# Attention values as 32-bit products in column halves, the causal mask on VectorE, and a mixed warm-up

## The chip, the core and the metric

The kernel runs on one core of a Trainium2 chip. A core has a matrix engine (TensorE, PE in the profile, with its weight loads listed as PEld), a vector engine (VectorE, DVE), an engine for activation functions and copies (ScalarE, ACT), a general engine (GpSimd, POOL) and a sync engine (SyncE, SP), which here issues nearly all DMAs. The engines run side by side, each in the order of its own queue, and wait for one another by semaphores. TensorE writes its products to PSUM (eight banks of 512 32-bit columns on 128 partitions); the other data sit in SBUF on 128 partitions.

The metric is the device time of one execution in microseconds. Before the change it is 1384.53 us, the median of three executions that lie between 1384.16 and 1384.84.

## The reference

One layer of a hybrid encoder for 1024 prompt frames and 32 frames of running streams that have 512 cached frames. All data are float32. Cut to what matters here:

```python
q, k, v, logf, ga, u, gb, ma, mb = mixer_inputs(x, ...)    # RMS norm and one wide projection
c = cumsum(logf)                                           # forget gates, per head
for i in range(T // 128):                                  # blocks of 128 queries
    s = q[block i] @ k[:hi].T + c[block i] - c[:hi]        # 16 heads of 64
    s = where(qpos >= kpos, s, -max)                       # causal mask
    o[block i] = softmax(s) @ v[:hi]
conv = causal_dwconv(u)                                    # 31 taps per channel
ya = (o * silu(ga)) @ w_pa
yb = (silu(layernorm(conv)) * silu(gb)) @ w_pb
y  = x + (sigmoid(ma) * ya + sigmoid(mb) * yb) @ w_out
```

Keys, values, log gates and the end of the convolution input are outputs too.

## The kernel before, in words

**Number formats.** A float32 product costs TensorE several passes. Most products here therefore take numbers in a rounded 32-bit format (the type `F32R`), which goes in one pass, and get their accuracy back by splitting an operand into a rounded high part and a low part (the rest), both of that type. A full product of two split operands is three one-pass products: high by high, low by high, high by low (`mms`, line 108).

**Stages.** The stages are: a start in which the tokens are normed and turned (`x_split`), with products on a zero tile ahead of it (`warm`, line 359) that keep TensorE occupied until the first tokens are there; projections for the convolution input, the values (line 600), keys and queries; a gate projection; then the attention stage; then the three output projections. The convolution taps run on VectorE beside the projections.

**Values in the projection stage.** For each group of four heads and each tile of 128 keys, ScalarE copies the values out of PSUM twice: as float32 (`vf`, line 606), which is stored as an output, and rounded (`vb`, line 608). Three steps later VectorE puts the low part beside the high one (line 613), and both are stored to `s_v` in DRAM, so that a key has 128 numbers per head: 64 high, 64 low.

**The attention stage.** `seq` holds 16 heads of 8 blocks (`Block(head, i)`: 128 queries, of which block i looks at i + 1 tiles of 128 keys), and four `Sample` items for the running streams, placed after block 0 of heads 3, 7, 11 and 15. TensorE's order is exactly the order of the loop (`manual_schedule`); the other engines' order is chosen by a planner. Iteration n of the loop does:

- `start(seq[n + 3])`, the scores of the block three further on: two products per half of the keys (lines 947 and 948) into one of two score buffers `psS` of two banks each, and then the mask as a bfloat16 product of an identity with a matrix of 0 and -1e30 on the last 128 keys (line 950). VectorE takes the row maximum (952), ScalarE the exponential and its row sum (955), GpSimd multiplies by the reciprocal (958).
- `turn()` of block n: TensorE transposes the probabilities in tiles of 128 (line 975) into a PSUM bank of the pool `psT` (three banks). ScalarE copies them out rounded (`pth`, 979), VectorE forms the low part (`ptl`, 980). Two blocks share one pair of tiles of 256 queries.
- `fill(4)`: four steps of a gate projection, of three 352-column products each (line 108). Eight steps make one chunk, whose result stands in the single bank of the pool `pq`; ScalarE copies it out (line 779) before the next chunk's first product may write there. So a chunk ends in every second fill. In head 8 three fills are left out.
- `values()` of block n - 2, for odd blocks alone: for the 256 queries of blocks i - 1 and i and for each of their key tiles, one product of V with `pth` and one with `ptl` (lines 991 and 992), 256 columns each. V is the stationary operand, 128 wide (64 high, 64 low), so the upper and lower 64 partitions of the result hold the two parts, which ScalarE (996) and VectorE (997) add into `ot`. For odd heads VectorE multiplies by the gate (1002), loaded when the head's first pair of blocks is done, and after block 7 the result is stored.

A head has 2 + 4 + 6 + 8 = 20 key tiles in its four pairs, so 40 value products; 16 heads have 640. V of the next head is loaded (one buffer) after the values of block 7.

Of the kernel before, what the change touches and what calls it, by code (L numbers as in the profile page):

```python
# [10 lines left out]
BF16 = mybir.dt.bfloat16  # L11
# [4 lines left out]
D = 1024  # L16
T = 1024
# [18 lines left out]
NWARM = 46  # L36
# [15 lines left out]
def build(tc, xT, xt, wv, wf, ckT, cv, clT, stT, vec, cst, yT, kT, vO, lfO, cpT, csT):  # L52
# [10 lines left out]
    s_v = dram.tile([8, 128, H, 128], F32, name="s_v")  # L63
# [281 lines left out]
    with tc.high_priority(offset=9000):  # L345
        nc.scalar.dma_start(cst_t[:, :C_CM], cst[:, :C_CM])
        load_tok(0)
        load_tok(1)
        nc.sync.dma_start(raws[0], wf[WIDX["ub", 0]])
        nc.sync.dma_start(vec_t, vec)  # L350
        nc.sync.dma_start(raws[1], wf[WIDX["ua", 0]])
        for t in range(2, 9):
            load_tok(t)
        nc.sync.dma_start(cst_t[:, C_CM:], cst[:, C_CM:])
        idle = xip.tile([128, CH], F32R, name="idle")
        nc.vector.memset(f32(idle), 0.0)
        warm = tr.tile([128, 512], F32, name="warm", tag="tr")
        for i in range(NWARM):
            nc.tensor.matmul(warm[:, :256], idle[:, :128], idle[:, :256], start=(i == 0), stop=(i == NWARM - 1))

# [7 lines left out]
    identb = cp.tile([128, 128], BF16, name="identb")  # L368
    cmaskb = cp.tile([128, 128], BF16, name="cmaskb")
# [115 lines left out]
    def consts():  # L485
        nc.vector.tensor_copy(smask, cst_t[:, C_SM:C_SM + TS])
        nc.vector.tensor_copy(identb, cst_t[:, C_ID:C_ID + 128])
        nc.vector.tensor_copy(cmaskb, cst_t[:, C_CM:C_CM + 128])
        nc.vector.tensor_copy(bones, cst_t[:, C_BO:C_BO + 128])
        nc.vector.tensor_scalar(qg8, vec_t[:, V_QG:V_QG + 1], 0.125, None, op0=ALU.mult)  # L490
# [86 lines left out]
    for c in range(4):  # L577
# [15 lines left out]
        for t in range(8):  # L593
# [18 lines left out]
            def low(ps=ps, vb=vb, t=t, c=c):  # L612
                nc.vector.tensor_sub(vb[:, :, 64:128], ps[:, :256].rearrange("p (h d) -> p h d", h=4),
                                     f32(vb[:, :, 0:64]))
                nc.sync.dma_start(s_v[t, :, 4 * c:4 * c + 4, :], f32(vb))

            later(3, low)
# [166 lines left out]
    class Head:  # L784
        def __init__(self, h):
            self.h = h

# [141 lines left out]
    class Block:  # L929
# [5 lines left out]
        def scores(self):  # L935
# [8 lines left out]
            for b in range(nb):  # L944
                last = b == nb - 1
                ksl = slice(b * w, b * w + wm)
                nc.tensor.matmul(ps[:, b, :wm], QB[:, qsl], KB[:, ksl], start=True, stop=False)  # L947
                nc.tensor.matmul(ps[:, b, :wm], QA[:, qsl], KA[:, ksl], start=False, stop=not last)  # L948
                if last:
                    nc.tensor.matmul(ps[:, b, w - 128:w], identb, cmaskb, start=False, stop=True)  # L950
# [9 lines left out]
        def turn(self):  # L960
            i, P = self.i, self.P
            if i % 2 == 0:
                tg = f"{(i // 2) % 2}"
                pth, ptl = [ap.tile([128, i + 2, 256], F32R, name=a, tag=a + tg, bufs=1) for a in ("pth", "ptl")]
                nc.gpsimd.memset(f32(pth[:, i + 1, 0:128]), 0.0)
                nc.gpsimd.memset(f32(ptl[:, i + 1, 0:128]), 0.0)
                self.head.p = pth, ptl
            self.p = self.head.p
            pth, ptl = self.p
            qo = slice((i % 2) * 128, (i % 2) * 128 + 128)  # L970
            for u in range((i + 4) // 4):
# [6 lines left out]
                js = slice(4 * u, 4 * u + nj)  # L978
                nc.scalar.copy(pth[:, js, qo], p3)  # L979
                nc.vector.tensor_sub(ptl[:, js, qo], p3, f32(pth[:, js, qo]))  # L980

        def values(self):
            if self.i % 2 == 0:
                return
            c, e = self.i // 2, self.head.h % 2
            pth, ptl = self.p
            V, ot = self.head.V, self.head.ot
            njb = 2 * c + 2
            po = psT.tile([128, 512], F32, name="po", tag="T")
            for j in range(njb):  # L990
                nc.tensor.matmul(po[:, :256], V[:, j, :], pth[:, j, :], start=(j == 0), stop=False)  # L991
                nc.tensor.matmul(po[:, :256], V[:, j, :], ptl[:, j, :], start=False, stop=(j == njb - 1))  # L992
            osl = slice(c * 256, c * 256 + 256)
            own = slice(64 * e, 64 * e + 64)
            oth = slice(64 - 64 * e, 128 - 64 * e)
            nc.scalar.copy(ot[own, osl], po[oth, :256])  # L996
            nc.vector.tensor_add(ot[own, osl], ot[own, osl], po[own, :256])  # L997
            if e == 1:
                if c == 0:
                    self.head.g = ap.tile([128, T], F32, name="ga", tag="kc", bufs=1)  # L1000
                    nc.sync.dma_start(self.head.g, s_g["ga"][self.head.h // 2, :, :T])
                nc.vector.tensor_mul(ot[:, osl], ot[:, osl], self.head.g[:, osl])
            if e == 1 and c == 3:
# [478 lines left out]
```

## Time and profile before

| What | Value |
|---|---|
| median of three executions | 1384.53 us |
| the profiled execution | 1384.38 us |
| its span, from the first to the last instruction | 1382.3 us |
| TensorE products busy | 1372.3 us (99%), 9478 instructions |
| VectorE busy | 975.5 us (71%) |
| ScalarE busy | 659.0 us (48%) |
| GpSimd busy | 654.7 us (47%) |
| attention stage, first to last value product | about 598 to 1088 us of the span |

The profile is a hardware trace of one execution. A group line reads: source line, engine, operation, tiles (`out<-in`), shapes, count, then busy time in us and mean duration of one in ns, then the idle time of the engine ahead of it and who ended it. In a timeline a row reads: start, duration, engine, line, operation, tiles, shapes, count. Products overlap one another in TensorE's pipeline, so the duration of one is longer than the time it takes from the next: to price a product in a stream, take the distance from its start to the next start.

### The profile page before, as it was taken

The numbers are of one execution on the slowest core, as the hardware profiler recorded it, in microseconds if no ns is written. First come the engines' busy times: TensorE is split into PE (matmuls) and PEld (weight loads), VectorE is DVE, ScalarE is ACT, GpSimd is POOL, SyncE is SP. The second block draws the span as 40 slices with busy tenths as digits, with TensorE's granted clock in tenths as the row PEclk, the third lists the DMA queues.
The fourth block names the chain that finished last, engine by engine and source line by source line (L and its number), as shares of the span: only waits on it lengthen the run. The fifth ranks groups of instructions, "written<-read, shape, count | busy, mean of one in ns | idle before, by whom it ended". The sixth has DMA issues, their size and how long they took to land.

```text
span 1382.3 us, 25127 instructions
## 1 busy us (share of the span) xinstructions
PE 1372.3 (99%) x9478; PEld 1333.4 (96%) x9478; DVE 975.5 (71%) x1368; ACT 659.0 (48%) x1346; POOL 654.7 (47%) x685
## 2 busy tenths in 40 slices
PE   8999999999999999999999999999999999999999
PEld 7999999999999999999999999999998999999999
DVE  6687788878898899747766667665454579255664
ACT  6333444556464642245555556655555566233320
POOL 2324244656585875453434343433433348355553
PEclk9999999999999999999999999999999999999999
DMA  5243442425242375245545456544552587634462
GB/s 214 63 174 124 147 144 93 154 70 168 94 158 94 118 195 162 77 136 151 152 124 163 126 171 173 143 136 138 151 153 94 181 318 258 210 110 138 138 202 68
DMA packets 113496, 203.36 MB, mean 147 GB/s; under 512 B 17696, under 2 KB 75936, under 8 KB 113376
## 3 DMA queue, kind: packets, MB, share of 16 engines
q1 hardware_dynamic: 113232, 201.70, 46.7%
q8 instruction: 75, 1.23, 0.4%
q14 instruction: 45, 0.37, 0.1%
q10 hardware_dynamic: 144, 0.07, 0.0%
HBM read 131.87 MB, written 69.84 MB: 146 GB/s over the span
## 4 chain that ended last, share of the span: by engine, by line
PE 95%; DMA 1%; DVE 1%; ACT 1%; issue 1%; POOL 0%; SPq 0%; ACTq 0%; POOLq 0%; DVEq 0%
PE pj L108 65%; PE pjv L600 7%; PE pj L1315 5%; PE ptr L975 5%; PE po L991 3%; PE po L992 3%; PE psS L947 3%; PE psS L948 2%; DMA xtok<-xt 1%; PE psS L950 1%; PE pst L724 1%; PE pst L723 1%; DMA raw<-wf 0%; PE ptx L442 0%; DMA u<-stT 0%
## 5 line engine op out<-in xcount | busy, mean ns | idle before, releaser
L108 PE MATMUL pj<-xh,wh 128*128 128x352 f32 (+2 forms) x1536 | 509.1, 331 | 1.7 <-ACT t L779 1.4
L108 PE MATMUL pj<-xl,wh 128*128 128x352 f32 (+2 forms) x1536 | 494.8, 322 | 0.2 <-DVE xl L445 0.2
L108 PE MATMUL pj<-xh,wl 128*128 128x352 f32 (+2 forms) x1536 | 493.1, 321 | 0.0
L100 POOL TENSOR_TENSOR wl<-raw,wh 128x384 fp32r<-128x384 f32 (+1 forms) x237 | 311.0, 1340 | 184.6 <-ACT wh L97 165.0
L272 DVE SCALAR_TENSOR_TENSOR y<-u,vec_t,y 128x1086 f32<-128x1086 f32 x240 | 378.4, 1577 | 11.5 <-ACT y L269 8.3
L108 PEld LDWEIGHTS pj<-xh,wh 128*128 128x128 f32 x1536 | 288.8, 188 | 4.7 <-ACT t L779 2.0
L108 PEld LDWEIGHTS pj<-xl,wh 128*128 128x128 f32 x1536 | 288.6, 188 | 1.4 <-DVE xl L445 1.2
L108 PEld LDWEIGHTS pj<-xh,wl 128*128 128x128 f32 x1536 | 289.2, 188 | 0.2 <-DVE wl L464 0.2
L958 POOL TENSOR_SCALAR P<-P,nm 128x128 f32<-128x128 f32 (+7 forms) x128 | 98.9, 773 | 228.8 <-DVE nm L957 195.8
L952 DVE TENSOR_REDUCE nm<-psS 128x1 f32<-128x128 f32 (+7 forms) x128 | 96.5, 755 | 72.2 <-PE psS L950 53.3
L979 ACT CAST pth<-ptr 128x512 fp32r<-128x512 f32 (+1 forms) x192 | 89.0, 481 | 81.6 <-PE ptr L975 81.3
L980 DVE TENSOR_TENSOR ptl<-ptr,pth 128x512 fp32r<-128x512 f32 (+1 forms) x192 | 103.3, 550 | 23.4 <-ACT pth L979 21.8
L97 ACT CAST wh<-raw 128x1024 fp32r<-128x1024 f32 x79 | 82.7, 1047 | 61.7 <-PE pj L108 28.5
L955 ACT ACTIVATE P<-psS,nm 128x128 f32<-128x128 f32 (+7 forms) x128 | 95.2, 744 | 35.0 <-DVE nm L952 31.4
L741 POOL TENSOR_TENSOR ql<-qn,qh 128x352 fp32r<-128x352 f32 (+1 forms) x48 | 64.3, 1340 | 69.1 <-ACT qh L740 59.8
L975 PE MATMUL ptr<-ident,P 128*128 128x128 f32 x576 | 85.0, 274 | 0.0
L991 PE MATMUL po<-pth,V 128*128 128x256 f32 x320 | 79.0, 283 | 0.0
L992 PE MATMUL po<-ptl,V 128*128 128x256 f32 x320 | 78.5, 281 | 0.0
L600 PE MATMUL pjv<-vwh,xh 128*128 128x260 f32 x256 | 72.5, 283 | 0.0
L600 PE MATMUL pjv<-vwl,xh 128*128 128x260 f32 x256 | 72.5, 283 | 0.0
L600 PE MATMUL pjv<-vwh,xl 128*128 128x260 f32 x256 | 72.3, 282 | 0.0
L997 DVE TENSOR_TENSOR ot<-ot,po 64x256 f32<-64x256 f32 x64 | 26.7, 417 | 59.9 <-ACT ot L996 59.2
(253 smaller groups left out, 2635.3 us busy)
## 6 DMA issues: line engine op xcount, KB each, us to landing
raw<-wf SPq DMA_DIRECT2D x92, 512.0 KB
s_v<-vb SPq DMA_DIRECT2D x32, 256.0 KB
QB<-s_q SPq DMA_DIRECT2D x32, 256.0 KB
KB<-s_k SPq DMA_DIRECT2D x32, 256.0 KB
V<-s_v SPq DMA_DIRECT2D x16, 512.0 KB
kT<-qn SPq DMA_DIRECT2D x8, 528.0 KB
s_ga<-t SPq DMA_DIRECT2D x24, 176.0 KB
s_gb<-t SPq DMA_DIRECT2D x24, 176.0 KB
```

The source lines that it names most:

```text
L100: nc.gpsimd.tensor_sub(wl[:, k0:k1, :], raw[:, k0:k1, :], f32(wh[:, k0:k1, :]))
L108: nc.tensor.matmul(ps, a[:, kt, :], b(kt, sl), start=(first and n == 0), stop=(last and n == N - 1))
L272: t = nc.vector.scalar_tensor_tensor(y, u[:, i:i + CW], w, y, op0=ALU.mult, op1=ALU.add)
L600: nc.tensor.matmul(ps[:, :VC], a, b, start=(n == 0), stop=(n == 23))
L952: nc.vector.tensor_reduce(nm[:, 0:1], ps[:, :nb, :w], axis=AX.XY, op=ALU.max, negate=True)
L955: nc.scalar.activation(P[:, :nk].rearrange("p (b w) -> p b w", b=nb), ps[:, :nb, :w], AF.Exp, bias=nm[:, 0:1], accum_out=nm[:, 1:2])
L958: nc.gpsimd.tensor_scalar(P[:, :nk], P[:, :nk], nm[:, 2:3], 1.0, op0=ALU.mult, op1=ALU.mult)
L975: nc.tensor.transpose(pt[:, 128 * j:128 * j + 128], P[:, 128 * (4 * u + j):128 * (4 * u + j) + 128], ident)
L979: nc.scalar.copy(pth[:, js, qo], p3)
L980: nc.vector.tensor_sub(ptl[:, js, qo], p3, f32(pth[:, js, qo]))
L991: nc.tensor.matmul(po[:, :256], V[:, j, :], pth[:, j, :], start=(j == 0), stop=False)
L992: nc.tensor.matmul(po[:, :256], V[:, j, :], ptl[:, j, :], start=False, stop=(j == njb - 1))
```

## The change

Four edits.

1. Values stay float32. The rounded copy `vb` and its low part are gone; `s_v` holds 64 numbers per key and head and is stored from `vf` at once. V is a float32 tile of 8 x 64.
2. The transposed probabilities stay float32, with one tile per pair of blocks (tag `pt0` with two buffers, `pt1` to `pt3` with one) instead of `pth` and `ptl`. They are copied out once: by ScalarE for the first four key tiles of a block, by VectorE for the others. All four pairs' value products come together at block 7: for key tile j one float32 product of V (64 wide) with 256 queries, into the lower 64 partitions for even j and into the upper 64 for odd j. The two PSUM banks taken hold two pairs each. Then the two partition halves are added, 512 queries at a time. The gate tile of an odd head is loaded at block 5.
3. The mask product is gone; VectorE adds a float32 mask to the last 128 key columns of the scores in PSUM, ahead of the row maximum.
4. The 46 warm-up products of 256 columns become 35 of 352, 256 and 512 columns, of two operands: the rounded 32-bit zero tile and a float16 zero tile.

```diff
-        for i in range(NWARM):
-            nc.tensor.matmul(warm[:, :256], idle[:, :128], idle[:, :256], start=(i == 0), stop=(i == NWARM - 1))
+        cold = xip.tile([128, 512], F16, name="cold")
+        nc.vector.memset(cold, 0.0)
+        kinds = [(idle, CH)] * 8 + [(cold, CH)] * 8 + [(idle, CH), (cold, CH)] * 4 + [(cold, 256)] * 6 + [(cold, 512)] * 5
+        for d, n in kinds:
+            nc.tensor.matmul(warm[:, :n], d[:, :128], d[:, :n], start=True, stop=True)
...
-            vb = vp.tile([128, 4, 128], F32R, name="vb", tag="vb", bufs=5)
-            nc.scalar.copy(vb[:, :, 0:64], ps[:, :256].rearrange("p (h d) -> p h d", h=4))
...
-            later(3, low)
+            nc.sync.dma_start(s_v[t, :, 256 * c:256 * c + 256], vf)
...
-            self.V = hp.tile([128, 8, 128], F32R, name="V", tag="V", bufs=1)
-            nc.sync.dma_start(f32(self.V), s_v[:, :, h, :].rearrange("b t d -> t b d"))
+            self.V = hp.tile([128, 8, 64], F32, name="V", tag="V", bufs=1)
+            nc.sync.dma_start(self.V, s_v[:, :, 64 * h:64 * h + 64].rearrange("b t d -> t b d"))
...
-                nc.tensor.matmul(ps[:, b, :wm], QA[:, qsl], KA[:, ksl], start=False, stop=not last)
-                if last:
-                    nc.tensor.matmul(ps[:, b, w - 128:w], identb, cmaskb, start=False, stop=True)
+                nc.tensor.matmul(ps[:, b, :wm], QA[:, qsl], KA[:, ksl], start=False, stop=True)
+            diag = ps[:, nb - 1, w - 128:w]
+            nc.vector.tensor_add(diag, diag, cmask)
...
             if i % 2 == 0:
-                tg = f"{(i // 2) % 2}"
-                pth, ptl = [ap.tile([128, i + 2, 256], F32R, name=a, tag=a + tg, bufs=1) for a in ("pth", "ptl")]
-                nc.gpsimd.memset(f32(pth[:, i + 1, 0:128]), 0.0)
-                nc.gpsimd.memset(f32(ptl[:, i + 1, 0:128]), 0.0)
+                c = i // 2
+                self.head.p[c] = ap.tile([128, i + 2, 256], F32, name="pt", tag=f"pt{c}", bufs=2 if c == 0 else 1)
+                nc.gpsimd.memset(self.head.p[c][:, i + 1, 0:128], 0.0)
...
-                nc.scalar.copy(pth[:, js, qo], p3)
-                nc.vector.tensor_sub(ptl[:, js, qo], p3, f32(pth[:, js, qo]))
+                (nc.vector.tensor_copy if u else nc.scalar.copy)(p[:, 4 * u:4 * u + nj, qo], p3)
 
         def values(self):
-            if self.i % 2 == 0:
+            if self.i == 5 and self.head.h % 2:
+                self.head.g = ap.tile([128, T], F32, name="ga", tag="kc", bufs=1)
+                nc.sync.dma_start(self.head.g, s_g["ga"][self.head.h // 2, :, :T])
+            if self.i < 7:
                 return
...
-            for j in range(njb):
-                nc.tensor.matmul(po[:, :256], V[:, j, :], pth[:, j, :], start=(j == 0), stop=False)
-                nc.tensor.matmul(po[:, :256], V[:, j, :], ptl[:, j, :], start=False, stop=(j == njb - 1))
+            pos = [psT.tile([128, 512], F32, name="po", tag="T") for _ in range(2)]
+            for c in range(4):
+                po = pos[c // 2][:, 256 * (c % 2):256 * (c % 2) + 256]
+                for j in range(2 * c + 2):
+                    rows = slice(64 * (j % 2), 64 * (j % 2) + 64)
+                    nc.tensor.matmul(po[rows], V[:, j, :], parts[c][:, j, :], start=(c % 2 == 0 and j < 2),
+                                     stop=(c % 2 == 1 and j >= 2 * c))
+            for u in range(2):
+                sl = slice(512 * u, 512 * u + 512)
+                nc.scalar.copy(ot[own, sl], pos[u][oth])
+                nc.vector.tensor_add(ot[own, sl], ot[own, sl], pos[u][own])
+                if e == 1:
+                    nc.vector.tensor_mul(ot[:, sl], ot[:, sl], self.head.g[:, sl])
```

In the small constants a float32 mask copy (`cmask`) takes the place of a bfloat16 identity and mask.

More of the change, by code (lines that the diff above doesn't have):

```diff
@@ L62, in build @@
     s_k = dram.tile([2, D, T], F32, name="s_k")
-    s_v = dram.tile([8, 128, H, 128], F32, name="s_v")
+    s_v = dram.tile([8, 128, D], F32, name="s_v")
     s_vs = dram.tile([TS, D], F32, name="s_vs")
@@ L367, in build @@
     smask = cp.tile([128, TS], F32, name="smask")
-    identb = cp.tile([128, 128], BF16, name="identb")
-    cmaskb = cp.tile([128, 128], BF16, name="cmaskb")
+    cmask = cp.tile([128, 128], F32, name="cmask")
     bones = cp.tile([128, 128], F32R, name="bones", tag="ob")
@@ L486, in consts @@
         nc.vector.tensor_copy(smask, cst_t[:, C_SM:C_SM + TS])
-        nc.vector.tensor_copy(identb, cst_t[:, C_ID:C_ID + 128])
-        nc.vector.tensor_copy(cmaskb, cst_t[:, C_CM:C_CM + 128])
+        nc.vector.tensor_copy(cmask, cst_t[:, C_CM:C_CM + 128])
         nc.vector.tensor_copy(bones, cst_t[:, C_BO:C_BO + 128])
@@ L993, in values @@
-            osl = slice(c * 256, c * 256 + 256)
+            e, V, ot, parts = self.head.h % 2, self.head.V, self.head.ot, self.head.p
             own = slice(64 * e, 64 * e + 64)
             oth = slice(64 - 64 * e, 128 - 64 * e)
-            nc.scalar.copy(ot[own, osl], po[oth, :256])
-            nc.vector.tensor_add(ot[own, osl], ot[own, osl], po[own, :256])
-            if e == 1:
[L999 to L1002, printed above, removed]
```

20 lines of the change are left out of this document (3 added, 17 removed).

## The prediction

> **What bounds the kernel now.** I read the page first: the share of each engine and the chain that ended last.
>
> ```profile
> span 1382.3 us, 25127 instructions
> PE 1372.3 (99%) x9478; PEld 1333.4 (96%) x9478; DVE 975.5 (71%) x1368; ACT 659.0 (48%) x1346; POOL 654.7 (47%) x685
> ...
> PE 95%; DMA 1%; DVE 1%; ACT 1%; issue 1%; POOL 0%; SPq 0%; ACTq 0%; POOLq 0%; DVEq 0%
> PE pj L108 65%; PE pjv L600 7%; PE pj L1315 5%; PE ptr L975 5%; PE po L991 3%; PE po L992 3%; PE psS L947 3%; PE psS L948 2%; DMA xtok<-xt 1%; PE psS L950 1%; PE pst L724 1%; PE pst L723 1%; DMA raw<-wf 0%; PE ptx L442 0%; DMA u<-stT 0%
> ```
>
> The chain is TensorE's own queue: 95% of it are its products, and no other engine holds more than 1%. The value products (L991, L992) are 3% each, the mask product (L950) 1%. A share is an average, so next I looked at a stretch of the attention stage, and at what TensorE waited for anywhere (us in total, times, longest).
>
> ```profile
> core 0: us, PE busy (x) PEld busy (x) DVE busy (x) ACT busy (x) POOL busy (x), PEclk, DMA share, GB/s
> ...
> 700.00:800.00 100.00, 100.00 (x735) 94.65 (x734) 70.32 (x131) 56.75 (x130) 38.78 (x70) 1.00 0.55 156
> ```
>
> ```profile
> PE ptx L442 <- DVE xl L445: 1.8, 2, 1.5
> PE pj L108 <- ACT t L779: 1.4, 2, 1.1
> ```
>
> In that stage TensorE has no gap, and the other engines have 30% or more to spare. The only engine that ever stops it there is ScalarE, when it is late in clearing the single bank of the gate projections (L779). So the time changes by what the change adds to and takes from TensorE's stream, plus new stops. Work taken from the other engines is worth nothing by itself.
>
> **What is removed.** Mean durations are of no use for prices here, since products overlap; I take distances between starts.
>
> ```profile
> L991 PE MATMUL po<-pth,V 128*128 128x256 f32 x320 | 79.0, 283 | 0.0
> L992 PE MATMUL po<-ptl,V 128*128 128x256 f32 x320 | 78.5, 281 | 0.0
> ...
> L950 PE MATMUL psS<-cmaskb,identb 128*128 128x128 bf16 x128 | 29.6, 231 | 0.0
> ```
>
> ```profile
> 848.60 0.23 PE L950 MATMUL psS<-cmaskb,identb 128*128 128x128 bf16 x1
> 848.67 0.39 PE L975 MATMUL ptr<-ident,P 128*128 128x128 f32 x2
> ...
> 849.01 0.29 PE L992 MATMUL po<-ptl,V 128*128 128x256 f32 x1
> ...
> 850.69 0.28 PE L992 MATMUL po<-ptl,V 128*128 128x256 f32 x1
> 850.81 0.75 PE L1025 MATMUL psn<-mean,ones_f 128*128 128x352 f32 x2
> ```
>
> From 849.01 to 850.81 lie 15 value products: 1.80 / 15 = 0.120 us each, and 640 of them 76.8 us. A mask product takes 0.07 us (848.60 to 848.67), 128 of them 9.0 us. Together 85.8 us leave the stream.
>
> **What is added: 320 float32 products in column halves.** The kernel has one burst that is built the same way: the running streams' values, float32 products of a 32-wide stationary operand into four different column quarters (line 557), 260 columns each.
>
> ```profile
> L557 PE MATMUL pjs<-vraw,xsm x64: 382/383/409, 68.6 to 158.2; 128*32 128x260 f32 x64
> ```
>
> The code has 32 such products and the trace 64 instructions, so a float32 product is two passes. How far the quarters run side by side is seen by ending the window of the timeline earlier and later (the duration is that of all passes begun by then):
>
> ```profile
> 68.60 0.43 PE L557 MATMUL pjs<-vraw,xsm 128*32 128x260 f32 x4
> ```
>
> ```profile
> 68.60 0.87 PE L557 MATMUL pjs<-vraw,xsm 128*32 128x260 f32 x12
> ```
>
> ```profile
> 68.35 0.32 PE L108 MATMUL pj<-xl,wh 128*128 128x352 f32 x1
> 68.60 1.09 PE L557 MATMUL pjs<-vraw,xsm 128*32 128x260 f32 x16
> 69.62 0.43 PE L108 MATMUL pj<-xh,wh 128*128 128x352 f32 x1
> 69.89 0.32 PE L108 MATMUL pj<-xh,wl 128*128 128x352 f32 x1
> ```
>
> Four passes begin together, and each further four add 0.22 us: (0.87 - 0.43) / 2. The passes of one quarter must follow one another, so 0.22 us is the time of one pass, and the four quarters run side by side. With 256 columns a pass takes 0.22 x 256 / 260 = 0.217 us, a product two passes, and a pair of products in two halves, if it overlaps like the quarters, 0.433 us. The change has 160 pairs (10 per head): 69.3 us. Not overlapped, the pair takes 0.867 us: 138.7 us. Those are the two ends; I take the lower, because the L557 rows are the same kind of instruction.
>
> On this the Trainium skill (TensorE: Matmul & The Clock Gate, section Part 3) has a measured table beside its model of full overlap: three column tiles ran only 2.38 times as fast as one. By 2.38 / 3, a pair would cost 0.546 us and all 87.3 us, and the sum below would end 18 us higher, at about 1394 us. The quarters above lose nothing inside the burst; what they lose is at its two ends.
>
> **The ends of a burst.** From 68.35 to 69.89 pass 1.54 us. Inside are four steps of 0.22 and two ordinary 352-column products of 0.16 (the step between rows further down: 930.35 to 930.51). What is left, 1.54 - 0.88 - 0.32 = 0.34 us, is the price of going into column tiles and out. Sixteen bursts: 5.4 us. Ends for this: 0 (the next work is let in early) to twice that, 10.9 us (a half is twice as wide as a quarter).
>
> **What the move of the value products uncovers.** A chunk of the gate projection ends in every second fill, and its bank must be cleared before the next fill. In heads 0 to 2 and from 12 on, the chunks end in even blocks, where no value products follow, before or after. Between the samples of heads 3 and 11 (a sample adds one fill; head 8 leaves three out) they mostly end in odd blocks, and there the value products cover the clearing:
>
> ```profile
> 930.35 0.33 PE L108 MATMUL pj<-xl,wh 128*128 128x352 f32 x1
> 930.51 0.28 PE L991 MATMUL po<-pth,V 128*128 128x256 f32 x1
> ...
> 930.71 0.45 ACT L779 COPY t<-pj 128x352 f32<-128x352 f32 x1 [0.83 <-PE pj L108]
> ...
> 931.93 0.34 PE L947 MATMUL psS<-KB,QB 128*128 128x384 f32 x1
> ...
> 932.29 0.23 PE L950 MATMUL psS<-cmaskb,identb 128*128 128x128 bf16 x1
> 932.36 0.28 PE L975 MATMUL ptr<-ident,P 128*128 128x128 f32 x1
> 932.39 0.41 PE L108 MATMUL pj<-xh,wh 128*128 128x352 f32 x1
> ```
>
> The bank is clear at 931.16, 0.81 us after the chunk's last product began, and was wanted at 932.39. After the change the 1.42 us of value products and the 0.07 of the mask are gone from this place: it is wanted 0.55 us after the last product, 0.26 too early, and with some 0.05 us for the signal TensorE stops for 0.31. Where the chunk ends in block 3 or 5, transposes and scores of 1.1 us or more remain; in block 1 the burst now covers it. Following the loop's order, the short place (after block 7, before a transpose of one tile) comes seven times, at 0.2 to 0.3 us: 1.8 us. In a few other places the cover is already near 0.86 us and the 0.07 of the mask comes back as a stop: 0.5 us. Together 2.3 us; ends 0 and 8.5 us (each of the seven with one ScalarE instruction of 0.9 us ahead of the copy: 7 x 1.21).
>
> **Mask and copies on VectorE.** The nearest row to the mask's addition (a 128x128 operation that reads PSUM) is the subtraction that goes away; the exponential of a six-tile block and the first product that reuses its score buffer give the room:
>
> ```profile
> L980 DVE TENSOR_TENSOR ptl<-ptr,pth 128x128 fp32r<-128x128 f32 x32 | 9.0, 280 | 0.2
> ```
>
> ```profile
> 944.25 0.90 ACT L955 ACTIVATE P<-psS,nm 128x768 f32<-128x768 f32 x1 [0.25 <-DVE nm L952]
> ...
> 949.80 0.48 PE L947 MATMUL psS<-KB,QB 128*128 128x512 f32 x1
> ```
>
> The addition is 128 x 0.28 = 36 us of VectorE work that lies in the chain scores, maximum, exponential. That chain frees its buffer 4.65 us before it is wanted (949.80 - 945.15), and three blocks of lead stand ahead of the transposes, so 0.28 us more costs nothing; without that cover it would cost up to 128 x 0.28. The bank that VectorE now writes is not one that TensorE is writing. VectorE loses all 192 subtractions and gets 64 copies, ScalarE loses 64 of its 192, GpSimd half its zero fills: none can become the bound at 70% busy. In the other direction nothing is gained either, since TensorE did not wait for them.
>
> **Edits that I cost at nothing.** The values' projection:
>
> ```profile
> L600 PE MATMUL pjv<-vwh,xh 128*128 128x260 f32 x256 | 72.5, 283 | 0.0
> ```
>
> TensorE has no gap ahead of these products, so the copies, subtractions and bytes that go away here free nothing; the store to `s_v`, now issued right behind the output's, waits for the same copy as that one, so SP's queue is not held longer. Loading V still waits for the last product of block 7, now 2.8 us later (4.7 against 1.9), but is wanted only at the next block 7; weight loads queued behind it on SP are fetched two thirds of a projection ahead. The gate tile is issued four iterations later and has two blocks left; if late, VectorE's multiplication waits, and behind it the row maxima, against the same 4.65 us. The two `po` banks leave one of the three `psT` banks for the next block's transposes, which need one. GpSimd's zero fill of `pt1` waits for the burst's products, which lie ahead of those transposes anyway.
>
> **The warm-up.** The 12 first of the 46 products, all of them, and what ends the wait after them:
>
> ```profile
> 1.29 2.93 PE L359 MATMUL warm<-idle 128*128 128x256 f32 x12 [1.29 <-DVE rs L377]
> ```
>
> ```profile
> 1.29 7.08 PE L359 MATMUL warm<-idle 128*128 128x256 f32 x46 [1.29 <-DVE rs L377]
> 8.22 1.32 DVE L414 TENSOR_SCALAR xtok<-xtok,rs 128x512 f32<-128x512 f32 x2
> 8.76 0.33 PE L442 MATMUL ptx<-ident,xtok 128*128 128x128 f32 x1 [0.40 <-DVE xtok L414]
> ```
>
> Before there are 46 x 256 = 11776 columns, after 24 x 352 + 6 x 256 + 5 x 512 = 12544. The first 3072 columns take 2.93 us (the slow clock of the start), the rest 4.15 / 34 / 256 = 0.48 ns a column. So the new one ends at 1.29 + 2.93 + 9472 x 0.00048 = 8.7 us, just before the tokens are ready at 8.76. I take 0. It can't gain, since VectorE ends that wait; it can lose up to 1 us, if each of the nine changes of type costs 0.11 us, the slower step after a burst (69.62 to 69.89 against 0.16).
>
> **The sum,** against the profiled execution, 1384.38 us (span 1382.3 and 2.1 around it; the median of 1384.53 is 0.15 higher): -76.8 - 9.0 + 69.3 + 5.4 + 2.3 + 0 = -8.8 us, so 1375.6 us. All free ends together (no price at the burst's ends, no stops) give -16.5: 1367.9 us. With the dear ends (10.9, 8.5, 1.0), but overlapped: +3.9: 1388.3 us.
>
> **The rivals.**
>
> 1. *The halves overlap incompletely.* It decides from 8.8 / 160 = 0.055 us per pair on: from there the kernel is slower. The mechanism would be that the 0.34 us is lost in part at every pair and not once a burst, because two tiles, each with two passes and two weight loads, leave the queue less to run ahead with than four. Half of it, 0.17 us, gives 27 us more: 1403 us; no overlap at all 1445 us. For it: no row shows halves. Against it: the steady 0.22 us steps. The 2.38 of the Trainium skill, named above, lies on this path. Chance 0.11.
> 2. *Stops take the gain.* ScalarE's copies out of the single bank come late in more places, or the planner, with other work to order, puts longer instructions ahead of them or of the maxima. The L779 row shows that such a stop exists already (1.1 us at worst); each of 16 heads would need 0.3 us and more beyond my count: 1380 to 1388 us. Chance 0.14, half of it still faster.
> 3. *The burst's ends cost nothing*, because the next scores start while the halves drain: 1368 to 1371 us. Chance 0.05.
>
> **How the numbers follow.** My forecast, 1371 to 1380 us, has 0.70. Some 0.2%, 2.8 us, is what a measurement here can tell from no change: 1381.8 to 1387.3 counts as the same. Faster: 0.70 + 0.07 + 0.05 = 0.82; the same 0.04 of rival 2; slower 0.11 + 0.03 = 0.14. The range runs from all free ends, 1367, to 1387, and leaves rival 1 out.
>
> **What will show it.** Right: 640 value passes of some 0.38 us in the trace, 16 bursts of 20 products of about 4.4 us each, the next product 0.3 us later than in a plain stream, no L950, and stops before L108 by L779 of some 2 to 4 us in all where 1.4 stood. Wrong: bursts of 5 us or more; starts of odd and even key tiles one after the other and not together; a stop of TensorE for VectorE's mask or maximum in the list of waits; transposes at the start later than 9.3 us.

## The result and the profile after

The changed kernel takes 1379.2 us, the median of six executions from 1379.09 to 1379.8; the kernel before, beside it, 1384.47 us. The ratio is 0.9962, with an interval of 0.9949 to 0.9975: faster by 5.3 us, where 8.8 were forecast. The profiled execution took 1379.15 us, its span 1377.3.

The page of the changed kernel: span, engines, the chain that ended last by engine and by line.

```profile
span 1377.3 us, 24403 instructions
...
PE 1366.6 (99%) x9339; PEld 1303.8 (95%) x9339; DVE 934.3 (68%) x1288; ACT 620.8 (45%) x1218; POOL 658.8 (48%) x621
...
PE 94%; DVE 2%; ACT 2%; issue 1%; DMA 1%; POOL 0%; SPq 0%; ACTq 0%; POOLq 0%; DVEq 0%
PE pj L107 64%; PE pjv L600 7%; PE pj L1303 5%; PE po L983 5%; PE ptr L964 5%; PE psS L939 3%; PE psS L940 2%; PE pst L716 1%; DMA s_q<-qh 1%; PE pst L715 0%; PE ptx L443 0%; DVE sql L708 0%; DMA xtok<-xt 0%; ACT xh L445 0%; PE pjs L557 0%
```

The values are 5% of the chain (3% and 3% before) and the mask product is gone. But VectorE and ScalarE have risen from 1% to 2%. By line, a DMA that stores queries (`s_q<-qh`) is new, and VectorE's `sql` now stands in the list: neither is in the attention stage. The waits of TensorE name the new ones (us in total, times, longest; these are the ones in the stages of keys, queries, gates and attention):

```profile
PE pj L107 <- ACT t L771: 1.1, 2, 0.8
PE pst L716 <- DVE sql L708: 0.9, 2, 0.6
...
PE psS L939 <- ACT t L769: 0.6, 1, 0.6
```

This list counts a wait only where TensorE ran dry. Products overlap, so a stop of 0.3 us hides in it: the gate copy has 1.1 us here and had 1.4 before, and the 2 to 4 us that the prediction gave as a sign do not show. The weight loads show the stops better. First the kernel before, then the changed one, from the groups of instructions by shape (busy us, mean ns, idle us before them and what ended it):

```profile
L108 PEld LDWEIGHTS pj<-xh,wh 128*128 128x128 f32 x1536 | 288.8, 188 | 4.7 <-ACT t L779 2.0 <-ACT xh L444 1.0 <-issue 0.8
```

```profile
L107 PEld LDWEIGHTS pj<-xh,wh 128*128 128x128 f32 x1536 | 288.5, 188 | 10.1 <-ACT t L771 6.5 <-issue 1.2 <-ACT xh L445 0.9
```

The idle time that ScalarE's copy of the gate projection ends has grown by 4.5 us.

To see where the 5 us of span come from, I cut the stream at the first product of each stage: the start up to the first values' projection; the projection of keys and queries (last values' product to last `pst` product); the gate projection to the first score product; the attention stage (to the first product of the output projection). The values' projection (119.28 us) and everything behind the attention stage (267.7 to 267.9) are alike in all kernels. The column of stops is part of the attention stage: the distances from a transpose to a gate product right behind it, less the 0.028 us that stands there without a stop (in most of the 111 to 126 such places). All are distances between starts of products in the trace, in us, of the one profiled execution of each kernel; the last column is the median of all executions. The experiments are explained below.

| kernel | start | keys, queries | gates | attention stage | stops at a gate product | median of runs (before, same chip) |
|---|---|---|---|---|---|---|
| before | 71.63 | 298.27 | 109.46 | 512.45 | 1.96 | 1384.47 |
| after | 71.59 | 299.69 | 110.22 | 505.26 | 4.66 | 1379.2 (1384.47) |
| mask only | 71.59 | 298.26 | 109.91 | 513.12 | 8.76 | 1386.6 (1384.08) |
| values only | 72.50 | 300.26 | 110.21 | 511.69 | 2.21 | 1385.88 (1384.08) |
| late loads | 71.93 | 298.27 | 110.22 | 505.11 | 4.65 | 1377.76 (1384.08) |
| burst early | 72.35 | 302.18 | 110.22 | 504.17 | 1.87 | 1378.18 (1384.08) |
| after, no mask | 71.97 | 299.67 | 110.22 | 502.46 | 2.26 | 1376.92 (1384.22) |
| before, no mask | 72.39 | 298.37 | 109.91 | 506.47 | 3.35 | 1377.68 (1384.22) |
| odd ends | 72.55 | 298.27 | 110.21 | 499.26 | 0.0 | 1372.36 (1384.22) |
| old warm-up | 72.47 | 298.29 | 110.21 | 505.13 | 4.62 | 1379.04 (1384.19) |
| mask, odd ends | 71.77 | 298.29 | 109.45 | 503.75 | 0.48 | 1376.54 (1384.19) |

The attention stage gained 7.19 us. Outside it the change lost 1.42 us among the keys and queries and 0.76 us at the end of the gates: 7.19 - 1.42 - 0.76 = 5.0, which is the gain of the span.

### The profile page after: what moved, and what is told of

The parts are those of the page before. It is cut to its first block, busy times and chain, and to the rows that moved or that the text cites. A ratio compares the mean times of both kernels' runs of the same rounds, so it can differ in the third digit from the quotient of the medians.

```text
span 1377.3 us, 24403 instructions
## 1 busy us (share of the span) xinstructions
PE 1366.6 (99%) x9339; PEld 1303.8 (95%) x9339; DVE 934.3 (68%) x1288; ACT 620.8 (45%) x1218; POOL 658.8 (48%) x621
## 4 chain that ended last, share of the span: by engine, by line
PE 94%; DVE 2%; ACT 2%; issue 1%; DMA 1%; POOL 0%; SPq 0%; ACTq 0%; POOLq 0%; DVEq 0%
PE pj L107 64%; PE pjv L600 7%; PE pj L1303 5%; PE po L983 5%; PE ptr L964 5%; PE psS L939 3%; PE psS L940 2%; PE pst L716 1%; DMA s_q<-qh 1%; PE pst L715 0%; PE ptx L443 0%; DVE sql L708 0%; DMA xtok<-xt 0%; ACT xh L445 0%; PE pjs L557 0%
## 5 line engine op out<-in xcount | busy, mean ns | idle before, releaser
L99 POOL TENSOR_TENSOR wl<-raw,wh 128x384 fp32r<-128x384 f32 (+1 forms) x237 | 316.1, 1361 | 205.0 <-ACT wh L96 179.9
L950 POOL TENSOR_SCALAR P<-P,nm 128x128 f32<-128x128 f32 (+7 forms) x128 | 108.0, 845 | 219.0 <-DVE nm L949 175.3
L967 ACT COPY pt<-ptr 128x512 f32<-128x512 f32 (+3 forms) x128 | 64.9, 507 | 78.6 <-PE ptr L964 77.9
L942 DVE TENSOR_TENSOR psS<-psS,cmask 128x128 f32<-128x128 f32 x128 | 38.0, 297 | 85.5 <-PE psS L940 84.4
L964 PEld LDWEIGHTS ptr<-ident,P 128*128 128x128 f32 x576 | 69.2, 140 | 5.3
L983 PE MATMUL po<-pt,V 128*64 128x256 f32 x640 | 72.6, 382 | 0.0
L949 DVE RECIPROCAL nm<-nm 128x1 f32<-128x1 f32 x128 | 20.3, 161 | 74.7 <-ACT P L947 74.5
```

Of the source, the lines that this page charges most:

```text
L99: nc.gpsimd.tensor_sub(wl[:, k0:k1, :], raw[:, k0:k1, :], f32(wh[:, k0:k1, :]))
L950: nc.gpsimd.tensor_scalar(P[:, :nk], P[:, :nk], nm[:, 2:3], 1.0, op0=ALU.mult, op1=ALU.mult)
L964: nc.tensor.transpose(pt[:, 128 * j:128 * j + 128], P[:, 128 * (4 * u + j):128 * (4 * u + j) + 128], ident)
L967: (nc.vector.tensor_copy if u else nc.scalar.copy)(p[:, 4 * u:4 * u + nj, qo], p3)
L983: nc.tensor.matmul(po[rows], V[:, j, :], parts[c][:, j, :], start=(c % 2 == 0 and j < 2), stop=(c % 2 == 1 and j >= 2 * c))
```

## The experiments

**One half only: do the halves run side by side?** All value products of a head go into the same half, so no pair can overlap; the copy and the addition of two halves become one copy.

```diff
-                    rows = slice(64 * (j % 2), 64 * (j % 2) + 64)
+                    rows = slice(64 * e, 64 * e + 64)
...
-                nc.scalar.copy(ot[own, sl], pos[u][oth])
-                nc.vector.tensor_add(ot[own, sl], ot[own, sl], pos[u][own])
+                nc.scalar.copy(ot[own, sl], pos[u][own])
```

> The changed kernel with all value products of a head in one column half, one after the other, and no addition of two halves. If the pairs run side by side in the changed kernel and not here, 160 x 0.433 = 69 us are added: about 1448 us. If the halves were side by side in name only, nothing is added: 1379 us.

Measured: 1448.18 us, ratio 1.0463 (1.0442 to 1.0484), 69 us above the changed kernel. TensorE's timeline (start, duration, count), a burst of the changed kernel and one of this:

```profile
993.40 0.32 PE L107 MATMUL pj<-xl,wh 128*128 128x352 f32 x1
993.65 4.54 PE L983 MATMUL po<-pt,V 128*64 128x256 f32 x40
998.12 0.45 PE L939 MATMUL psS<-KB,QB 128*128 128x384 f32 x1
998.40 0.34 PE L940 MATMUL psS<-KA,QA 68*128 68x384 f32 x1
```

```profile
705.98 8.85 PE L983 MATMUL po<-pt,V 128*64 128x256 f32 x40
714.76 0.42 PE L939 MATMUL psS<-KB,QB 128*128 128x320 f32 x1
```

From the first of 40 passes to the next product pass 998.12 - 993.65 = 4.47 us with two halves and 714.76 - 705.98 = 8.78 us with one: 0.22 us for a pass by itself, and 0.22 us for two in two halves. They run side by side almost without loss: 8.78 / 4.47 = 1.96. So the first rival is out, and with it the figure of the Trainium skill (TensorE: Matmul & The Clock Gate, section Part 3), 2.38 for three tiles, as a price for this kernel; that table is for another shape, which no run here tries.

**The mask alone, and the values alone.** The first puts the mask's addition into the kernel before; the second puts the mask product back into the changed one.

```diff
-                if last:
-                    nc.tensor.matmul(ps[:, b, w - 128:w], identb, cmaskb, start=False, stop=True)
+            diag = ps[:, nb - 1, w - 128:w]
+            nc.vector.tensor_add(diag, diag, cmask)
```

> The kernel before, with the mask added by VectorE and nothing else changed. Theory A (the mask's 0.3 us lies in front of ScalarE's exponentials, and so delays copies out of the gates' single bank): TensorE loses 128 mask products, 9.3 us, and gets some 2 us of new stops at L779 or its like, 1.4 us in the list of waits becomes 3 to 4; about 1377 us. Theory B (the mask on VectorE is hidden, as predicted, and the missing gain lies in the value products): 1375.2 us and no new stops.

> The changed kernel with the mask as a bfloat16 product again. Theory A: 9.3 us of products come back, but the six stops of 0.26 us and the one of 1.0 us ahead of the gates' first product go: about 1386 us, slower than before by 1 to 2 us. Theory B: the stops stay, 1388.5 us.

Measured: the mask alone takes 1386.6 us, ratio 1.0017 (1.0007 to 1.0026), slower, where a gain of some 7 us was expected. The values alone take 1385.88 us, ratio 1.0013 (1.0003 to 1.0022), slower too, as expected. Each part by itself loses some 2 us, and both together gain 5.3. For the attention stage the table has +0.7, -0.8 and, together, -7.2 us.

The waits of the mask-only kernel, and its weight loads:

```profile
PE pj L108 <- ACT t L777: 5.3, 11, 1.4
...
PE psS L944 <- ACT P L952: 1.7, 2, 1.5
```

```profile
L108 PEld LDWEIGHTS pj<-xh,wh 128*128 128x128 f32 x1536 | 288.5, 188 | 13.6 <-ACT t L777 10.0 <-ACT xh L443 0.9 <-issue 0.8
```

Idle time that the gate copy ends is 10.0 us here against 2.0 before; by the table the stops at gate products rise from 1.96 to 8.76 us. One such place, VectorE and ScalarE:

```profile
1024.62 0.30 DVE L947 TENSOR_TENSOR psS<-psS,cmask 128x128 f32<-128x128 f32 x1
1024.95 0.29 DVE L977 TENSOR_TENSOR ptl<-ptr,pth 128x128 fp32r<-128x128 f32 x1
1025.16 0.41 DVE L999 TENSOR_TENSOR ot<-ot,ga 128x256 f32<-128x256 f32 x1
1025.49 0.68 DVE L949 TENSOR_REDUCE nm<-psS 128x1 f32<-128x512 f32 x1
1026.27 0.69 ACT L952 ACTIVATE P<-psS,nm 128x512 f32<-128x512 f32 x1 [1.60 <-DVE nm L949]
1026.95 0.44 ACT L777 COPY t<-pj 128x352 f32<-128x352 f32 x1
```

The same place in the kernel before:

```profile
1023.99 0.69 DVE L952 TENSOR_REDUCE nm<-psS 128x1 f32<-128x512 f32 x1
...
1024.71 0.29 DVE L980 TENSOR_TENSOR ptl<-ptr,pth 128x128 fp32r<-128x128 f32 x1
1024.78 0.69 ACT L955 ACTIVATE P<-psS,nm 128x512 f32<-128x512 f32 x1 [0.66 <-DVE nm L952]
...
1024.92 0.42 DVE L1002 TENSOR_TENSOR ot<-ot,ga 128x256 f32<-128x256 f32 x1
...
1025.71 0.45 ACT L779 COPY t<-pj 128x352 f32<-128x352 f32 x1 [0.15 <-PE pj L108]
```

Before, the maximum comes first and the low part and the gate's multiplication follow it. With the addition the planner puts these two between the addition and the maximum, so the maximum starts 0.87 us after the addition and not 0.3. In 58 of the 128 blocks of the mask-only kernel other work of VectorE stands between the two; in the changed kernel, which has no low parts, in 33. ScalarE stands 1.60 us waiting for the maximum, and the copy that clears TensorE's bank stands behind the exponential in ScalarE's order. At the gate products TensorE does not wait for the maximum itself; it waits for what is queued behind it. (The 1.5 us of `psS <- ACT P` are another way: behind a sample, at 828.8 us, the exponential freed its score buffer too late.)

**Without the mask: what does VectorE's addition cost?** The addition is left out, so the mask is not applied: first in the changed kernel, then in the mask-only kernel.

```diff
-            nc.vector.tensor_add(diag, diag, cmask)
```

> The changed kernel with VectorE's addition of the mask left out, so the scores are not masked; nothing else is changed. Theory A (the 0.3 us of the addition delays the exponentials that stand ahead of the copies out of the gates' bank): the stops of 0.26 us after block 4 and the one of 1.0 us go, 2.6 us less than the changed kernel, about 1376.2 us. Theory C (the planner's order of ScalarE does it, whatever VectorE takes): 1378.8 us.

> The kernel before without its mask products and with nothing in their place, so the scores are not masked. Theory A: 9.3 us of products go and few stops come: about 1375 to 1376 us, 11 us under the kernel that adds the mask on VectorE. Theory C (the stops come with any order of ScalarE that the planner makes when the mask product is gone): 1383 to 1386 us, like that kernel.

Measured: 1376.92 us, ratio 0.9947 (0.9932 to 0.9962), and 1377.68 us, ratio 0.9951 (0.9934 to 0.9968). So the addition, with the order of VectorE's work that comes with it, costs 1379.2 - 1376.92 = 2.3 us in the changed kernel (2.8 in the attention stage: 505.26 - 502.46; 2.0 if each median is set against the kernel before beside it) and 1386.6 - 1377.68 = 8.9 us in the old one (6.65 in the stage of the profiled executions). The old kernel with neither product nor addition gained 6.0 us of stage and not the 9.3 that the products took: part of them was cover for the gate copies, whose stops rise by 1.4 us to 3.35, and 0.9 us are a wait for a load of V.

The place of the loss in the changed kernel, a fill after block 4 in which a chunk ends:

```profile
1005.89 1.23 DVE L944 TENSOR_REDUCE nm<-psS 128x1 f32<-128x1024 f32 x1
...
1007.23 1.12 ACT L947 ACTIVATE P<-psS,nm 128x1024 f32<-128x1024 f32 x1 [0.72 <-DVE nm L944]
...
1007.60 0.32 PE L107 MATMUL pj<-xl,wh 128*128 128x352 f32 x1
...
1008.34 0.44 ACT L771 COPY t<-pj 128x352 f32<-128x352 f32 x1
...
1008.83 0.43 PE L107 MATMUL pj<-xh,wh 128*128 128x352 f32 x1
```

The same place without the addition:

```profile
976.93 1.12 ACT L946 ACTIVATE P<-psS,nm 128x1024 f32<-128x1024 f32 x1 [0.38 <-DVE nm L943]
977.63 0.33 PE L107 MATMUL pj<-xl,wh 128*128 128x352 f32 x1
...
978.04 0.45 ACT L771 COPY t<-pj 128x352 f32<-128x352 f32 x1
...
978.60 0.41 PE L107 MATMUL pj<-xh,wh 128*128 128x352 f32 x1
```

The copy begins 0.74 us after the chunk's last product with the addition and 0.41 us without; the next chunk starts 1.23 us after that product with it, 0.97 us without: 0.26 us. The exponential of 1024 columns waits 0.72 against 0.38 us for the maximum, and the copy is next in ScalarE's order. Six places after block 4 stop for 0.26 us and one (652.2) for 1.0; without the addition the six are gone and the one is down to 0.26. These are 2.3 of the difference of the stops, 4.66 - 2.26 = 2.4 us; four stops of 0.15 us and less go as well, and one of 0.29 comes.

**Late loads: the loss ahead of the attention stage.** In the changed kernel the planner issues the loads of heads 0 and 1 in the middle of the projection of keys and queries. The issues of `QB`, before and after (duration in ns, first and last start in us):

```profile
L794 SPq DMA_DIRECT2D QB<-s_q x16: 450/451/583, 502.8 to 1008.9; - x16
```

```profile
L787 SPq DMA_DIRECT2D QB<-s_q x16: 450/451/514, 320.2 to 1005.2; - x16
```

SP's queue, ScalarE and TensorE of the changed kernel there:

```profile
323.85 0.38 SPq L734 DMA_DIRECT2D s_q<-qh  x1
324.28 0.48 SPq L791 DMA_DIRECT2D QA<-s_q  x1
...
328.95 0.40 SPq L801 DMA_DIRECT2D V<-s_v  x1
330.26 0.35 SPq L734 DMA_DIRECT2D s_q<-qh  x1
...
330.87 0.49 ACT L732 CAST qh<-qn 128x352 fp32r<-128x352 f32 x1 [3.09 <-DMA s_q<-qh]
...
339.62 0.43 PE L716 MATMUL pst<-sql,bones 128*128 128x352 f32 x1 [0.55 <-DVE sql L708]
```

The stores of the keys and queries stand in SP's queue between the loads. ScalarE waits 3.09 us for a `qh` buffer that such a store is to free, the one issued at 323.85, and TensorE runs dry soon after. The experiment ties the loads of these two heads to a `silu` of the gate projection, so that they come behind the keys and queries (those of head 0 from 561.9 us on).

```diff
+            if h < 2:
+                for t in loads:
+                    tc.add_manual_dep(t.ins, sides["silu"].ins.name, ...)
```

> The changed kernel, where the loads of the first two heads may not be planned ahead of the gate projection. Theory A (the planner moved them from 503 to 320 us of the span, where they hold up the stores of keys and queries, and with them ScalarE): the stops of 0.7 and 0.6 us ahead of the second product of the norms' sums go, and the span is 1.4 to 2.1 us shorter: about 1377.1 to 1377.8 us. Theory B (the stores would be late there anyway): 1379.2 us.

Measured: 1377.76 us, ratio 0.9953 (0.9939 to 0.9968), 1.4 us better than the changed kernel, as expected (1.0 if each is set against the kernel before beside it; the intervals of the two ratios overlap); the keys and queries are back at 298.27. What the early loads cost differs from one execution to the next: 1.4 us in the profiled execution of the changed kernel, 2.0 with the values alone, 3.9 in the next experiment, and 0.0 with the old warm-up, although SP issues the same DMAs in the same order in all four up to there, the loads from 320.2 to 320.6 us on. From the issue of that store to ScalarE's next copy into `qh` pass 7.0 us in the changed kernel (323.85 to 330.87), 6.7 with the old warm-up and 8.3 with the burst early. Why the planner finds room for the loads earlier was not tested. The loss of 0.76 us at the end of the gates (the wait L939 <- L769 above) stays here. Every kernel with the new values has it: there the first score product starts when ScalarE's last `silu` of the gate projection has ended. With the old values it starts ahead of that `silu`, and the loss is 0.0, or 0.45 at two gate products earlier on. What ties the product to the `silu` stays open.

**The burst early: the seven short places.** The value products of block 7 move up, between the next block's transposes and its fill, so that they cover the clearing of the bank; the gate tile and V are loaded earlier to match.

```diff
             b.turn()
+            if b.i == 0 and n:
+                seq[n - 1].values()
             fill(4 if b.i > 2 or b.head.h != 8 else 0)
```

> The changed kernel with a head's burst of value products one iteration earlier, ahead of the fill of the next head's block 0, and the gate tile loaded at block 3. Theory A (seven places where nothing covers the copy out of the gates' bank after block 7): those stops of 0.2 to 0.3 us go, 1.7 us in all: about 1377.5 us. Theory B (the copies are late there for another reason, ScalarE's order): 1379.2 us.

Measured: 1378.18 us, ratio 0.9961 (0.9946 to 0.9976): not told apart from the changed kernel. In the trace the seven stops after block 7 are gone (1.87 us of stops in all, and the six after block 4 among them). The stops are 2.8 us less, but the attention stage is only 1.1 us shorter: among others a product that waits for its weights (at 1096.6 us, 0.9 us late) and a score product that waits for its buffer (853.8, 0.8 us late) are new. The early loads cost 3.9 us in the profiled execution instead of 1.4; it took 1381.42 us and the other three 1377.68 to 1378.49, so it stands for itself alone.

**Odd ends: all three together.** Late loads and the early burst, and the chunks are shifted: a fill of eight steps before the loop and none at the samples, so that chunks end in odd blocks throughout.

```diff
-    fill(4)
+    fill(8)
...
         if isinstance(b, Sample):
-            fill(4)
             b.turn()
         else:
             b.turn()
-            fill(4 if b.i > 2 or b.head.h != 8 else 0)
+            if b.i == 0 and n:
+                seq[n - 1].values()
+            fill(4 if b.i > 1 or b.head.h != 8 else 0)
```

> The changed kernel with the late loads, with the burst ahead of the fill of the next head's block 0, and with the chunks of the gate projections ending in odd blocks throughout: the second fill of the stage has eight steps, the samples have none, head 8 leaves out two fills and not three. Theory A: no load is early (1.2 us), the stops after block 7 (1.7 us) and those after block 4 (1.6 us) are gone: about 1374.5 us. If ScalarE is late in odd blocks too, up to 1377 us.

Measured: 1372.36 us, ratio 0.9915 (0.99 to 0.993): 11.9 us faster than the kernel before and 6.8 faster than the changed one, the best of this study, and 2 us better than expected. Its weight loads:

```profile
L107 PEld LDWEIGHTS pj<-xh,wh 128*128 128x128 f32 x1536 | 288.8, 188 | 8.6 <-issue 6.2 <-ACT xh L445 0.7 <-ACT t L771 0.6
```

The idle time that the gate copy ends is 0.6 us where 6.5 stood. (The 6.2 of "issue" did not stop the products: by the table no gate product is late any more, and the stage is 6.0 us shorter than in the changed kernel: 4.7 are the stops, and 1.2 lie between score products, which mostly no longer follow a burst.)

**The mask alone in odd ends.** The same shift of the fills in the mask-only kernel, nothing else.

> The kernel before with the mask added by VectorE, its value products as they were, and the chunks of the gate projections ending in odd blocks throughout (second fill of eight steps, none in the samples, two left out in head 8). Theory A (the mask on VectorE costs only where the copy out of the gates' bank has short cover, after even blocks): the 9.3 us of mask products come out of the time and the stops of the mask-only kernel go: about 1375 us. If VectorE's own load keeps the copies late, little changes against that kernel: 1383 us or more.

Measured: 1376.54 us, ratio 0.9944 (0.9928 to 0.9961), 10 us better than the mask alone:

```profile
L108 PEld LDWEIGHTS pj<-xh,wh 128*128 128x128 f32 x1536 | 288.6, 188 | 4.3 <-ACT t L777 1.0 <-ACT xh L443 0.9 <-issue 0.8
```

The mask's addition is as long as in the mask-only kernel (0.29 us), but where a chunk ends other work now stands ahead of the next chunk; 10.0 us of idle time have become 1.0. So most of what the addition cost went through the gate copies behind it; the odd ends without any mask were not run. What is left: transposes of this kernel wait 2.0 us for VectorE, in three places at 826 to 863 us, which they do not in the kernel before; whether that comes from the addition was not tested. The longest:

```profile
PE ptr L972 <- DVE ot L994: 1.1, 1, 1.1
```

**The old warm-up** in the changed kernel:

> The changed kernel with the 46 warm-up products of 256 columns of before. If the new warm-up costs and gains nothing, as predicted: about 1378.8 us, the same as the changed kernel within 0.3 us, and the first gate product of the trace starts within 0.1 us of where it does there (10.27 us).

Measured: 1379.04 us, ratio 0.9961 (0.9946 to 0.9976), like the changed kernel. The start column of the table runs from 71.59 to 72.47 with the old warm-up and from 71.59 to 72.55 with the new one: it differs from execution to execution, not by kernel. The first gate product starts at 10.40 us, 0.13 after that of the changed kernel, where at most 0.1 was expected; but with the new warm-up alone it lies between 10.27 and 10.76. The trace of this run cannot be read finer than about a microsecond, since in its profiled execution the start was late (72.47) and the early loads cost nothing.

## Why the prediction came out as it did

The direction and the main mechanism, pairs that run side by side, were right: 1379.2 us against 1375.6, inside the range. In the span the change gained 5.0 us where the sum had 8.8. Point by point:

- *Value products and the ends of a burst* (-76.8 + 69.3 + 5.4 = -2.1): right, -1.7 measured. The value products took 76.6 us. Now a burst passes 4.47 us from its first pass to the next product, 16 x 4.47 = 71.5, and 3.4 more lie outside: 0.25 instead of 0.16 into the burst, 0.28 instead of 0.18 between the two scores behind it, and 0.2 instead of 0.03 where a burst stands behind a sample's transpose. Undisturbed steps are 0.2155 us (narrow windows of the timeline), 20 x 16 of them 69.0; the rest, 71.5 + 3.4 - 69.0 = 5.9, is 0.37 per burst where 0.34 was read from the four quarters. The third rival, ends that cost nothing, is out.
- *The mask product* (-9.0): -8.6. Its 9.3 us are gone, but the product behind the scores now starts 0.7 us later in sum.
- *Stops at gate products* (+2.3): +2.7 by the table, but not of the parts foreseen. The seven short places are right in place and size: 0.21 to 0.32 us each, 1.7 in all (predicted 1.8). One of them:

```profile
723.30 0.32 PE L107 MATMUL pj<-xl,wh 128*128 128x352 f32 x1
723.66 0.45 ACT L771 COPY t<-pj 128x352 f32<-128x352 f32 x1 [1.05 <-PE pj L107]
723.92 0.27 PE L964 MATMUL ptr<-ident,P 128*128 128x128 f32 x1
724.16 0.43 PE L107 MATMUL pj<-xh,wh 128*128 128x352 f32 x1
```

  That the total is so near the forecast is luck. The "few other places" (0.5) did not come. The one large stop of the old kernel, 1.4 us at 1050.7, where a sample's exponential stood ahead of the copy, is gone, which was not foreseen. And 2.4 us are the next point.
- *The addition on VectorE* (0): here the prediction failed at "0.28 us more costs nothing". The size was right:

```profile
L942 DVE TENSOR_TENSOR psS<-psS,cmask 128x128 f32<-128x128 f32 x128 | 38.0, 297 | 85.5 <-PE psS L940 84.4
```

  But its cover was checked for two users of the chain alone, the score buffer (4.65 us) and the transposes (three blocks). What was missed stands in ScalarE's order: the gate copy behind the exponential, with nearly no cover. It costs 2.3 us of time. The second rival's first half, copies that come late in more places, came true here.
- *Edits costed at nothing*: failed as well, with 2.2 of the 3.8 us that are missing. That is about as much as the addition's 2.4, most of which was offset by stops that were counted and did not come or that went unforeseen. The loads of heads 0 and 1 are no part of the diff; the planner issued them 180 us sooner, for 1.42 us in this execution. The 0.76 us at the end of the gates was not foreseen either. The second rival had named "the planner, with other work to order": it came true in a small size, outside the stage for which it was meant.
- *Warm-up* (0): right as far as can be told. In the profiled execution the first transpose came at 8.82 us (8.76 before); in the other profiled executions it came at 9.15 to 9.82 with the new warm-up and at 8.84 to 9.50 with the old. The "slow clock of the start" is not shown: the first products are slow, but the profile has a granted clock of 1.00 over the first 10 us.

With the measured terms the sum is -1.7 - 8.6 + 2.7 + 1.42 + 0.76 = -5.4; the span says -5.0, so 0.4 us of small distances are unassigned.

The losses of the two parts by themselves follow from the table. Values alone: -0.8 in the stage and +0.75 at the gates, together nothing; the loss is +2.0 from early loads and a start that was 0.9 late in the profiled execution, and both differ between executions. Mask alone: the 9.3 us are eaten by 6.8 more of stops at gate products, the 1.7 of wait at `psS` and some 1.5 in smaller distances, and the kernel ends above the one before. The place shown above gives the reason: there VectorE has the old work between the addition and the maximum. In the changed kernel the new values take much of that work away. That this is what makes the difference was not tested by itself. So, it seems, the prediction's "Work taken from the other engines is worth nothing by itself" holds in the kernel before; it no longer holds once the mask moves to VectorE, where the same addition costs 8.9 us with the old values and 2.3 with the new ones.

## What to carry to other kernels

Before a step on a side engine is costed at nothing, follow its chain to every reader, and on each engine also to the next instruction in that engine's order: the loss came from a copy that uses nothing of the lengthened chain and merely stands behind it. Two edits that touch the same engine are to be priced together, and tried apart and together: here each alone was slower, the values alone, by their trace, only through early loads and a late start, and both were faster. And where a single bank is cleared at fixed points of the stream, move those points to where other work covers the clearing; with the burst moved and the loads held back this was worth 6.8 us, where the change itself was worth 5.3.

## What the hardware showed beside that

Pairs of float32 passes in two column halves run as fully side by side as four in quarters: one pass 0.22 us, two 0.22, four 0.22. The cost lies at the ends of the burst: 0.34 us with the quarters, 0.37 with the halves.

The start differs between profiled executions. The granted clock from 20 to 24 us was 0.57 in the profiled execution with the old warm-up and 1.00 in that of the changed kernel (window and its length, PE, PEld, DVE, ACT and POOL busy, granted clock, DMA share, GB/s):

```profile
20.00:24.00 4.00, 4.00 (x22) 4.00 (x21) 3.63 (x8) 3.60 (x8) 0.00 (x0) 0.57 0.38 130
```

```profile
20.00:24.00 4.00, 4.00 (x32) 3.96 (x32) 3.33 (x7) 3.88 (x9) 0.00 (x0) 1.00 0.31 101
```

A clock of 0.57 to 0.61 there occurred in five of the twelve profiled executions, with the old and the new warm-up alike, and these five are the ones whose first values' product came at 72.35 us or later (72.35 to 72.55; the others 71.59 to 72.07). The start alone can so differ by nearly 1 us, more than several of the terms weighed here, and a reason to compare single traces stage by stage and not by their spans.
